# z of six head pairs of an attention layer as seven half-size products ahead of the attention loop

## The chip, the cores and the metric

The kernel runs on one core of one Trainium2 chip. The metric is device time in microseconds (us) of one execution. The engines are PE (TensorE, the matrix unit), DVE (VectorE), ACT (ScalarE), POOL (GpSimd) and SP (SyncE, which issues the DMA transfers). Each engine runs its own instructions in order and waits on semaphores for the others.

## What is computed

Two layers over 640 tokens: 512 of a prompt, and 8 samples of 16. Layer 0 is a gated MLP with a spatial mix (`gmlp_branch`); layer 1 is attention with a forget bias. The prompt attends to itself, the samples to 256 cached rows and to their own. z gates the attention's output by silu. Each layer ends with an output product, a residual with norms and a gated embedding. Cut to layer 1:

```python
proj = h @ w_in
q = proj[..., :E]; k = proj[..., E:2 * E]; v = proj[..., 2 * E:3 * E]
z = proj[..., 3 * E:4 * E]
logf = jax.nn.log_sigmoid(proj[..., 4 * E:] + b_f)
# prompt and samples, per head:
s = q @ k.T * scale + cT[q_pos] - cT[k_pos]      # cT: cumulative sum of logf
y = softmax(where(k_pos <= q_pos, s, -inf)) @ v
out = (y * jax.nn.silu(z)) @ w_out
```

D_MODEL is 1024, E 2048, and there are 16 heads of 128, worked on in eight pairs.

## The kernel before

**Products.** The precision is float32. Each operand is split into a high and a low fp32r part, and each product is three matmuls (`mm3`, L249 to L251: high by high, high by low, low by high). The activations of a layer, transposed and split, stand in A (`h_at`, `quarter`): 8 row tiles by 640 tokens. In the channel form (`channel_steps`) a 128x128 weight tile stands in PE and the 640 tokens pass in pieces of 384 and 256 columns.

**Seven products.** For a pair (256 output channels) the weights are cut into 2x2 blocks of four 128x128 tiles and the activations into 2x2 blocks of 320 tokens (`quarter`). `seven_products` (L523) forms the product of the two from seven products of blocks, or of sums of blocks, where the plain way takes eight: 7 x 4 tiles x 3 = 84 matmuls of 320 columns. The four sums of weights (left operands) are added by GpSimd in `left_operands` (L191 to L199); the sums of activations (right operands) are made once in `right_operands`, and the results are added on DVE (L531 to L546). Before, layer 0 alone does so, for its u and z.

**Weights.** `units` lists all weight pieces in the order of use. `fetch` loads them (512 KB each) into RAW, three slots. `split` makes the high part on ACT (L263) and the low part on DVE (L264) and puts them in W.

**Layer 1.** `project(p, parts)` makes v, k, q and z of head pair p. It is a generator, and `interleave` runs it and starts given pieces of attention at planned times. Pair 0 is projected first (with the forget logits, their logarithm and sums beside it). Then a loop over p = 0 to 6 projects pair p + 1 while pair p attends; the last pass has no z, since z of pair 7 is made behind the loop, with the last pair's attention and `tail(1)`, the output product. A pass of p = 0 to 5 has a planned length of 57 and steps of 5.6, the last one 43 and 4.2.

**Attention.** Per head, four row blocks of the prompt: scores on PE, softmax on DVE and ACT (its last step, the division by the row sum, is L955 before and L979 after), transposes on PE (L961 before, L985 after), values on PE (L968). For the samples, `load_k` brings cached K, 16 loads of 128 KB for a pair, and DVE transposes it (`turn_k`, L1000 before and L1024 after). K, V and the broadcast rows of c (the cumulative sums, through c_sc in DRAM) stand in one tile, r2b_t (`second`), 10240 columns wide. The results of a pair go to DRAM (y_sc) and come back for the tail.

**Queues.** Nearly all transfers are issued by SP (`dma`, L118 to L119), in order: a load that waits for its place holds up all that stand behind it. The scheduler that builds the program reorders instructions on each engine by its own estimate of time, so the order of rows decides what stands behind a wait.

Of the kernel before, what the change touches and what calls it, by code (L numbers as in the profile page):

```python
# [56 lines left out]
def hybrid_trunk(tc, x_prompt, x_sample, ck, cv, clf, p_prompt, p_sample, norm_pre, norm_post,  # L58
# [27 lines left out]
    c_sc = dram.tile([H, SEQ], F32, name="c_sc")  # L86
    cs_sc = dram.tile([P, 272], F32, name="cs_sc")
# [66 lines left out]
    for p in range(8):  # L154
        for part in (2, 1, 0, 3):
            for kk in range(2):
                u_rows(f_win[0], kk * 512, part * E + p * 256, 4, 256)
    u_tail(f_wout, 1)
# [15 lines left out]
    state = {"raw": 0, "used": 0}

    def raw_of(i):
        if S0 <= i < S1:
            z = (i - S0 + 1) % 4
            if z == NRAW:
                return r1(o_X, 1024)  # L180
        else:
            z = i % NRAW if i < S0 else (i + 1) % NRAW
        return RAW[:, z * 1024:z * 1024 + 1024]
# [7 lines left out]
    def left_operands(i, j):  # L191

        (a11, a21), (a12, a22) = ([raw_of(r).rearrange("p (k n) -> p k n", k=4)[:, :, z:z + P] for z in (0, P)] for r in (i, i + 1))
        s2, s3, s1, s4 = (SF[:, z * 512:z * 512 + 512].rearrange("p (k n) -> p k n", k=4) for z in range(4))
        if j == 0:
            for o, a, b, op in ((s1, a21, a22, ALU.add), (s2, s1, a11, ALU.subtract), (s3, a11, a21, ALU.subtract),
                                (s4, a12, s2, ALU.subtract)):
                nc.gpsimd.tensor_tensor(out=o, in0=a, in1=b, op=op)
# [186 lines left out]
    o_X, o_ln, o_sum, o_th = 14208, 15232, 16256, 17216  # L385
# [4 lines left out]
    SF = pool2.tile([P, 2560], F32, name="sf")  # L390

# [6 lines left out]
    b11, b12, b21, b22, t_a, t_b = (r1(10240 + z * 1280, 1280).rearrange("p (k n) -> p k n", k=4) for z in (0, 1, 2, 3, 4, 0))  # L398

    def right_operands():  # L400

        for q, (i, j) in zip((b11, b12, b21, b22), ((0, 0), (0, 1), (1, 0), (1, 1))):
            hi, lo = quarter(i, j)
            nc.vector.tensor_tensor(out=q, in0=f(hi), in1=f(lo), op=ALU.add)
        for o, a, b, dst in ((t_a, b12, b11, 0), (t_b, b22, t_a, 1), (b21, b21, t_b, 2), (b12, b22, b12, None)):
            nc.vector.tensor_tensor(out=o, in0=a, in1=b, op=ALU.subtract)
# [27 lines left out]
    for p in range(4):  # L434
# [4 lines left out]
        for kk in range(4):  # L439
# [20 lines left out]
    fetch(S0 + 4)  # L460
# [25 lines left out]
    assert o_A + 256 <= o_X  # L486
# [66 lines left out]

    def eight_products(done):
        wz = weights(2)
        for i in range(2):
            for j, o in enumerate(channel_unit(wz, i, UZ)):
                done(i, j, o[:, :HT])
# [32 lines left out]
    for g in range(0, 16, 2):  # L591
        for part, finish in ((0, finish_u), (1, finish_z)):
            if 2 * part in SEVEN:
                seven_products(lambda i, j: uv_of(g + i)[part][:, HALF[j]], lambda i, j, c: finish(g, i, j, c))
            else:
                eight_products(lambda i, j, c: finish(g, i, j, c))
# [174 lines left out]
    assert o <= 7168  # L771
# [112 lines left out]
    def project_q(p):  # L884
        ws = weights(2)
        for hh in range(2):
# [6 lines left out]
                                    scalar1=scale, scalar2=None, op0=ALU.mult)  # L893

# [258 lines left out]
```

## Time and profile before

| | |
|---|---|
| median of 3 runs (lowest to highest) | 1331.51 us (1331.37 to 1331.73) |
| the profiled execution: its own time | 1330.92 us |
| its span in the trace | 1329.1 us |
| busy: PE, DVE, ACT, POOL | 1319.5, 767.0, 542.6, 136.1 us |
| moved by DMA | 172.87 MB, 299913 packets, 188769 of them under 512 bytes |

The profile is one execution taken by the hardware profiler. PE is busy nearly all the time. Layer 0 reaches to about 540 us, pair 0 of layer 1 is projected up to about 600 us, the loop runs from there to about 1106 us, six passes of about 74 us and one of 60, and the rest is the last pair and the tail. PE's records of matmuls have modelled ends, so the time of one matmul is read from the distance of two starts. PEld is the loading of weights, which lies beside PE's work.

### The profile page before, as it was taken

How to read it: one execution, taken by the hardware profiler on the slowest of the kernel's cores; microseconds unless marked ns; L12 is line 12 of the kernel's file. 1: busy time of each engine (PE TensorE's matmuls, PEld its weight loads, DVE VectorE, ACT ScalarE, POOL GpSimd, SP SyncE). 2: the span in 40 equal slices, each digit the busy share in tenths (PEclk: the TensorE clock that was granted, in tenths of full speed). 3: DMA queues.
4: the chain of work that ended last, by engine and by line, in shares of the span. 5: the costliest groups of instructions: out<-in, count | busy, mean ns of one | idle time of the engine just before them, and what ended most of it. 6: DMA issues, size and time to landing. Idle time of an engine off the chain costs nothing.

```text
span 1329.1 us, 21541 instructions
## 1 busy us (share of the span) xinstructions
PE 1319.5 (99%) x8363; PEld 1191.4 (90%) x8363; DVE 767.0 (58%) x1581; ACT 542.6 (41%) x1025; POOL 136.1 (10%) x144
## 2 busy tenths in 40 slices
PE   9999999999999999999999999999999999999998
PEld 6888999999888788999999999999999998888786
DVE  7744999998844546545545454544545465544642
ACT  5434555444544334424333333433334344445341
POOL 1012454443000100000000000000000000000100
PEclk9999999999999999999999999999999999999999
DMA  6432343322424204689778675778778687243211
GB/s 224 137 101 69 119 129 102 106 85 73 139 86 151 79 26 120 184 141 170 124 163 165 153 165 140 157 153 163 122 148 173 149 211 244 92 149 112 64 64 48
DMA packets 299913, 172.87 MB, mean 130 GB/s; under 512 B 188769, under 2 KB 269201, under 8 KB 299810
## 3 DMA queue, kind: packets, MB, share of 16 engines
q1 hardware_dynamic: 299666, 171.23, 52.0%
q8 instruction: 65, 1.06, 0.3%
q14 instruction: 38, 0.31, 0.1%
q10 hardware_dynamic: 144, 0.26, 0.1%
HBM read 149.86 MB, written 21.59 MB: 129 GB/s over the span
## 4 chain that ended last, share of the span: by engine, by line
PE 97%; DVE 2%; DMA 0%; issue 0%; ACT 0%; SPq 0%; POOL 0%; DVEq 0%
PE pb L249 29%; PE pb L251 28%; PE pb L250 28%; PE pb L968 3%; PE pb L961 1%; PE pb L1022 1%; PE pb L1048 1%; PE pb L287 1%; PE pb L568 1%; DVE W L264 1%; PE pb L1045 1%; DMA RAW<-in_gmlp_w_in 0%; PE pb L1040 0%; DVE R L576 0%; PE pb L569 0%
## 5 line engine op out<-in xcount | busy, mean ns | idle before, releaser
L249 PE MATMUL pb<-A,W 128*128 128x384 f32 (+2 forms) x1024 | 330.4, 323 | 0.0
L251 PE MATMUL pb<-A,W 128*128 128x384 f32 (+2 forms) x1024 | 317.5, 310 | 0.0
L250 PE MATMUL pb<-A,W 128*128 128x384 f32 (+2 forms) x1024 | 316.8, 309 | 0.0
L249 PE MATMUL pb<-W,A 128*128 128x512 f32 (+1 forms) x840 | 298.2, 355 | 2.1 <-ACT R L694 1.4
L251 PE MATMUL pb<-W,A 128*128 128x512 f32 (+1 forms) x840 | 293.6, 351 | 0.6 <-DVE A L264 0.6
L250 PE MATMUL pb<-W,A 128*128 128x512 f32 (+1 forms) x840 | 294.1, 350 | 0.0
L264 DVE TENSOR_TENSOR W<-RAW,W 128x1024 fp32r<-128x1024 f32 (+1 forms) x156 | 193.2, 1239 | 151.2 <-ACT W L263 148.6
L263 ACT ACTIVATE W<-RAW 128x1024 fp32r<-128x1024 f32 (+1 forms) x156 | 161.2, 1033 | 155.4 <-PE pb L250 70.2
L249 PEld LDWEIGHTS pb<-A,W 128*128 128x128 f32 x1024 | 193.0, 188 | 7.5 <-issue 6.8
L250 PEld LDWEIGHTS pb<-A,W 128*128 128x128 f32 x1024 | 193.1, 189 | 0.7
L251 PEld LDWEIGHTS pb<-A,W 128*128 128x128 f32 x1024 | 192.6, 188 | 0.4 <-issue 0.4
L249 PEld LDWEIGHTS pb<-W,A 128*128 128x128 f32 x840 | 159.1, 189 | 26.5 <-issue 3.1
L251 PEld LDWEIGHTS pb<-W,A 128*128 128x128 f32 x840 | 158.9, 189 | 21.2 <-DVE A L264 0.9
L250 PEld LDWEIGHTS pb<-W,A 128*128 128x128 f32 x840 | 159.0, 189 | 20.1 <-issue 0.4
L264 DVE TENSOR_TENSOR A<-R,A 128x640 fp32r<-128x640 f32 (+1 forms) x51 | 41.0, 835 | 74.2 <-ACT A L263 71.9
L1000 DVE STREAM_TRANSPOSE r2b_t<-r2b_t 128x256 f32<-128x256 f32 x128 | 46.3, 412 | 34.4 <-PE pb L1022 26.1
L263 ACT ACTIVATE A<-R 128x640 fp32r<-128x640 f32 (+1 forms) x51 | 36.7, 747 | 67.6 <-PE pb L250 65.6
L249 PE MATMUL pb<-tb,W 128*128 128x320 f32 x192 | 59.7, 311 | 0.4
L251 PE MATMUL pb<-tb,W 128*128 128x320 f32 x192 | 59.3, 309 | 0.0
L250 PE MATMUL pb<-tb,W 128*128 128x320 f32 x192 | 59.3, 309 | 0.0
L273 POOL TENSOR_TENSOR SML<-SML 128x1 f32<-128x1 f32 x25 | 17.5, 701 | 385.4 <-DVE SML L271 380.7
L963 ACT ACTIVATE R<-pb 128x128 f32<-128x128 f32 (+1 forms) x64 | 27.9, 437 | 65.5 <-PE pb L961 65.3
(235 smaller groups left out, 1865.6 us busy)
## 6 DMA issues: line engine op xcount, KB each, us to landing
RAW<-in_fox_w_in SPq DMA_DIRECT2D x64, 512.0 KB
RAW<-in_gmlp_w_in SPq DMA_DIRECT2D x40, 512.0 KB
r2b_t<-in_cache_fox_v SPq DMA_DIRECT2D x32, 512.0 KB
r2b_t<-in_cache_fox_k SPq DMA_DIRECT2D x128, 128.0 KB
RAW<-in_gmlp_w_out SPq DMA_DIRECT2D x16, 512.0 KB
RAW<-in_ple_w_gate SPq DMA_DIRECT2D x16, 512.0 KB
RAW<-in_fox_w_out SPq DMA_DIRECT2D x16, 512.0 KB
out<-R SPq DMA_DIRECT2D x40, 128.0 KB
```

The lines of the kernel that those rows point to most:

```text
L249: nc.tensor.matmul(out, lh, rh, start=start, stop=False)
L250: nc.tensor.matmul(out, lh, rl, start=False, stop=False)
L251: nc.tensor.matmul(out, ll, rh, start=False, stop=stop)
L263: nc.scalar.activation(out=hi, in_=src, func=AF.Copy)
L264: nc.vector.tensor_tensor(out=lo, in0=src, in1=f(hi), op=ALU.subtract)
L273: nc.gpsimd.tensor_tensor(out=q, in0=t, in1=mhalf, op=ALU.pow)
L287: nc.tensor.transpose(out=b[:, j * P:(j + 1) * P], in_=src[:, (4 * c + j) * P:(4 * c + j + 1) * P], identity=ident)
L568: nc.tensor.matmul(b0[:, t * P:(t + 1) * P], v_at(pnl, t)[:, c0:c0 + P], wm, start=True, stop=True)
L961: nc.tensor.transpose(out=tb[:, j * P:(j + 1) * P], in_=pr[:, j * P:(j + 1) * P], identity=ident)
L963: nc.scalar.activation(out=pt[:, :n], in_=tb[:, :n], func=AF.Copy)
L968: nc.tensor.matmul(O[:, d], v[:, j, hh * P:(hh + 1) * P], pt[:, j * P:(j + 1) * P], start=(j == 0), stop=(j == i))
L1000: nc.vector.transpose(out=kt[:, hh, bl, :PAST], in_=kr[:, hh, bl])
```

## The change

z of pairs 1 to 6 is made by seven half-size products in `make_z`, pair after pair, ahead of the loop, and stored to DRAM (z_sc, 655 KB for a pair). `z_again` loads it in the pass that uses it, and the loop's projections have v, k and q alone; each pass has the length 43 and steps of 4.2. z of pair 0 is made by eight products as before, but right behind v and k, and q of pair 0 comes behind `make_z(6)`. z of pair 7 stays. In particular:

- `units` has the weights in the new order; `SEVEN` names two stretches of it where weights are split as sums and a fourth RAW slot is used.
- `right_operands` is called a second time, beside the projection of pair 0, with its four additions on GpSimd. It makes four sums (a fourth takes the place of a quarter that layer 0 replaces) in r2k_t, which stands where r2b_t stands later: r2b_t comes only when the last seven products have read it.
- The left sums go to R1, as do the forget gate's temporaries, which stood in r2b_t.
- The forget logits and their logarithm come at 24.0 and 30.0 of pair 0's projection and the sums behind z of pair 2. K of pair 0 is loaded in the first pass, not beside pair 0's projection.

```diff
-    for p in range(8):
-        for part in (2, 1, 0, 3):
+    def u_pair(p, parts):
+        for part in parts:
             for kk in range(2):
                 u_rows(f_win[0], kk * 512, part * E + p * 256, 4, 256)
+
+    u_pair(0, (2, 1, 3))
+    Z0 = len(units)
+    for p in range(1, 7):
+        u_pair(p, (3,))
+    Z1 = len(units)
+    u_pair(0, (0,))
+    for p in range(1, 8):
+        u_pair(p, (2, 1, 0) if p < 7 else (2, 1, 0, 3))
...
-    S0, S1 = 16, 48
-    SEVEN = (0, 2)
+    SEVEN = ((16, 48, 14208), (Z0, Z1, 13504))
...
-    def right_operands():
-
+    def right_operands(base, t3, eng):
+
+        b11, b12, b21, b22 = (r1(base + z * 1280, 1280).rearrange("p (k n) -> p k n", k=4) for z in range(4))
         for q, (i, j) in zip((b11, b12, b21, b22), ((0, 0), (0, 1), (1, 0), (1, 1))):
             hi, lo = quarter(i, j)
-            nc.vector.tensor_tensor(out=q, in0=f(hi), in1=f(lo), op=ALU.add)
-        for o, a, b, dst in ((t_a, b12, b11, 0), (t_b, b22, t_a, 1), (b21, b21, t_b, 2), (b12, b22, b12, None)):
+            eng.tensor_tensor(out=q, in0=f(hi), in1=f(lo), op=ALU.add)
+        for o, a, b, dst in ((b11, b12, b11, 0), (b12, b22, b12, t3), (b22, b22, b11, 1), (b21, b21, b22, 2)):
             nc.vector.tensor_tensor(out=o, in0=a, in1=b, op=ALU.subtract)
             if dst is not None:
                 split(*right_sum(dst), o)
+        return b12
...
-    pool2, R2 = second("r2b", F32)
+    pool2, TB = second("r2k", F32R)
+    state["sums"] = r1(10496, 2048)
...
+    def make_z(p):
+
+        zst = r1((7456, 15168)[p % 2], 2 * TOK)
+
+        def into(i, j):
+            return zst[:, i * TOK:(i + 1) * TOK][:, HALF[j]]
+
+        def done(i, j, c):
+            th = r1(14528 + j * HT, HT)
+            nc.scalar.activation(out=th, in_=c, func=AF.Tanh, scale=0.5)
+            nc.vector.scalar_tensor_tensor(out=into(i, j), in0=th, scalar=1.0, in1=c, op0=ALU.add, op1=ALU.mult)
+
+        seven_products(into, done, right_sum(3), 12544)
+        dma(z_sc[2 * p:2 * p + 2].rearrange("h p t -> p h t"), zst.rearrange("p (h t) -> p h t", h=2))
+
+    def z_again(p):
+        dma(r1(RA + (p % 2) * 4608 + 3328, 2 * TOK).rearrange("p (h t) -> p h t", h=2), z_sc[2 * p:2 * p + 2].rearrange("h p t -> p h t"))
...
-    PARTS = (project_v, project_k, project_q, project_z)
-    interleave(project(0, PARTS), [(0.0, forget_logits), (6.0, log_forget), (20.0, forget_sums), (30.0, lambda: load_k(0, 0))])
+    PARTS = (project_v, project_k, project_q)
+    interleave(project(0, (project_v, project_k, project_z)),
+               [(8.0, lambda: right_operands(12544, 3, nc.gpsimd)), (24.0, forget_logits), (30.0, log_forget)])
+    for p in range(1, 7):
+        make_z(p)
+        if p == 2:
+            forget_sums()
+    pool2.release()
+    pool2, R2 = second("r2b", F32)
+    run(project_q(0))
+    length, step = 43, 4.2
     for p in range(7):
-        length, step = (57, 5.6) if p < 6 else (43, 4.2)
-        pieces = kv_times(p, 0, 5) + kv_times(p, 1, length / 2) + sample_times(p, 0, 5) + sample_times(p, 1, length / 2)
-        pieces += [(2, lambda p=p: load_k(p, 1)), (length / 2 - 3, lambda p=p: load_k(p + 1, 0))]
+
+        t0, t1 = (12, 27) if p == 0 else (5, length / 2)
+        pieces = [(t0 - 14, lambda p=p: z_again(p))] if p else [(0, lambda: load_k(0, 0))]
+        pieces += kv_times(p, 0, t0) + kv_times(p, 1, t1) + sample_times(p, 0, t0) + sample_times(p, 1, t1)
+        pieces += [(t0 - 3, lambda p=p: load_k(p, 1)), (t1 - 3, lambda p=p: load_k(p + 1, 0))]
         for hh in range(2):
             pieces += prompt_times(2 * p + hh, 2 + 4 * step * hh, step)
-        interleave(project(p + 1, PARTS if p < 6 else PARTS[:3]), pieces)
+        interleave(project(p + 1, PARTS), pieces)
         store_y(p)
```

How the change moves rows is shown at two places (line, operation, tiles, shape; R_69 is the tile R1, pb is a PSUM bank, "waits" names the engine or DMA lane that a row waits for).

The first is SP's queue where the first cached K is loaded, before, beside pair 0's projection (c_sc and cs_sc hold the cumulative sums):

```order
L119 DMA r2b_t<-in_cache_fox_k 32x32x32 x4
L119 DMA RAW<-in_fox_w_in 128x4x256
L119 DMA r2b_t<-c_sc 128x512
L119 DMA R_69<-cs_sc 128x1x272
L119 DMA r2b_t<-in_cache_fox_k 32x32x32 x4
L119 DMA RAW<-in_fox_w_in 128x4x256
L119 DMA r2b_t<-c_sc 128x512
L119 DMA R_69<-cs_sc 128x1x272
```

and after, from the last weights of `make_z` to the first pass:

```order
L121 DMA RAW<-in_fox_w_in 128x4x256
L121 DMA r2b_t<-c_sc 128x512
L121 DMA r2b_t<-in_cache_fox_k 32x32x32 x5
L121 DMA z_sc<-R_69 128x2x640
L121 DMA r2b_t<-in_cache_fox_k 32x32x32 x3
L121 DMA r2b_t<-c_sc 128x512
L121 DMA r2b_t<-in_cache_fox_v 128x4x256 x2
L121 DMA RAW<-in_fox_w_in 128x4x256
L121 DMA r2b_t<-in_cache_fox_k 32x32x32 x4
L121 DMA r2b_t<-in_cache_fox_v 128x4x256
L121 DMA R_69<-z_sc 128x2x640
L121 DMA r2b_t<-in_cache_fox_k 32x32x32 x4
```

The sixteen K loads of pair 0, with c, V and the reload of z, now stand one behind the other behind the last product that reads r2k_t; before, they were spread over the projection of pair 0 and the first pass.

The second is DVE at the transposes of cached K. Before, the first ones stood beside splits of weights (L264) of pair 0:

```order
L264 TENSOR_TENSOR W<-R_69,W 128x512 [waits Activation_49]
L1000 STREAM_TRANSPOSE r2b_t<-r2b_t 128x256 [waits DMAHW2_49,DMAHW7_49,DMAHW1_49,DMAHW0_49]
L809 COPY r2b_t<-pb_74 16x512 [waits PE_49]
L819 COPY r2b_t<-pb_75 128x272 [waits PE_49]
L1000 STREAM_TRANSPOSE r2b_t<-r2b_t 128x256 [waits DMAHW2_49,DVE_49]
L1000 STREAM_TRANSPOSE r2b_t<-r2b_t 128x256
L264 TENSOR_TENSOR W<-RAW,W 128x1024 [waits DMAHW4_49,PE_49,Activation_49]
L1000 STREAM_TRANSPOSE r2b_t<-r2b_t 128x256 [waits DMAHW3_49,DVE_49]
L264 TENSOR_TENSOR W<-RAW,W 128x1024 [waits PE_49,Activation_49]
L1000 STREAM_TRANSPOSE r2b_t<-r2b_t 128x256 [waits DMAHW6_49,DMAHW7_49,DMAHW5_49,DMAHW0_49]
L1000 STREAM_TRANSPOSE r2b_t<-r2b_t 128x256
```

After, those for the second half of the samples stand between the parts of a softmax of the prompt (L975 to L979) and the samples' scores (L1049):

```order
L972 ISA SML 128x1
L975 TENSOR_SCALAR SML<-SML 128x1 [waits DVE_49]
L1024 STREAM_TRANSPOSE r2b_t<-r2b_t 128x256 [waits DMAHW4_49,DMAHW3_49,DMAHW5_49,DMAHW2_49,PE_49]
L978 RECIPROCAL SML<-SML 128x1 [waits Activation_49]
L1024 STREAM_TRANSPOSE r2b_t<-r2b_t 128x256 [waits PE_49] x3
L1024 STREAM_TRANSPOSE r2b_t<-r2b_t 128x256 [waits DMAHW2_49,DMAHW1_49,DMAHW3_49,DMAHW0_49,PE_49]
L979 TENSOR_SCALAR R_69<-R_69,SML 128x384 [waits DVE_49]
L1049 ISA R_69,SML<-pb_74,R_69 128x272 [waits PE_49,Pool_49]
L1049 ISA SML 128x1
L1024 STREAM_TRANSPOSE r2b_t<-r2b_t 128x256 x3
L279 TENSOR_TENSOR W<-RAW,W 128x1024 [waits Activation_49]
```

The division L979, which the transposes L985 on PE wait for, now has the last two groups of K transposes ahead of it, each with a wait for four DMA lanes; the next split of weights (L279, L264 before) stands behind them.

More of the change, by code (lines that the diff above doesn't have):

```diff
@@ L86, in hybrid_trunk @@
     c_sc = dram.tile([H, SEQ], F32, name="c_sc")
+    z_sc = dram.tile([H, P, TOK], F32, name="z_sc")
     cs_sc = dram.tile([P, 272], F32, name="cs_sc")
@@ L153, in hybrid_trunk @@
     u_tail(g_wout, 0)
-    for p in range(8):
-        for part in (2, 1, 0, 3):
+    def u_pair(p, parts):
+        for part in parts:
             for kk in range(2):
                 u_rows(f_win[0], kk * 512, part * E + p * 256, 4, 256)
+    u_pair(0, (2, 1, 3))
[6 more added lines that the diff above has]
+        u_pair(p, (2, 1, 0) if p < 7 else (2, 1, 0, 3))
+    n1 = len(units)
     u_tail(f_wout, 1)
-    S0, S1 = 16, 48
-    SEVEN = (0, 2)
+    SEVEN = ((16, 48, 14208), (Z0, Z1, 13504))
     items = []
+    raw_slot, raw_last = [], [-1] * (NRAW + 1)
+    part_of = {}
     for i in range(len(units)):
-        if not S0 <= i < S1 or i % 4 - i % 2 not in SEVEN:
+        part = next((x for x in SEVEN if x[0] <= i < x[1]), None)
+        if part is None:
             items.append((i, None))
-        elif i % 2 == 0:
+        elif i % 2 == part[0] % 2:
             items += [(i, j) for j in range(4)]
-    n0 = S1 + 16 + 2 + 8
-    few = range(n0, n0 + 64 + 12)
+            part_of[i] = part
+        if part and i == part[0]:
+            raw_last[NRAW] = i
+        z = min(range(NRAW + (part is not None)), key=lambda z: raw_last[z])
+        raw_last[z] = i
+        raw_slot.append(RAW[:, z * 1024:z * 1024 + 1024] if z < NRAW else r1(part[2], 1024))
+    few = range(Z1, n1 + 12)
     place, last_use = [], [-1] * (2 * NW)
-    state = {"raw": 0, "used": 0}
+    state = {"raw": 0, "used": 0, "sums": None}
     def raw_of(i):
[L177 to L183, printed above, removed]
+        return raw_slot[i]
     def fetch(upto):
@@ L193, in left_operands @@
         (a11, a21), (a12, a22) = ([raw_of(r).rearrange("p (k n) -> p k n", k=4)[:, :, z:z + P] for z in (0, P)] for r in (i, i + 1))
-        s2, s3, s1, s4 = (SF[:, z * 512:z * 512 + 512].rearrange("p (k n) -> p k n", k=4) for z in range(4))
+        sf = state["sums"]
+        s2, s3, s1, s4 = (sf[:, z * 512:z * 512 + 512].rearrange("p (k n) -> p k n", k=4) for z in range(4))
         if j == 0:
@@ L305, in hybrid_trunk, with channel_steps @@
     SPLITS = ((0, SA), (SA, TOK))
-    def channel_steps(ws, hh, banks, splits=SPLITS):
+    def channel_steps(ws, hh, banks):
         out = [bank(banks), bank(banks)]
@@ L311, in channel_steps @@
             w = [z[:, k % 4, hh * P:(hh + 1) * P] for z in ws[k // 4]]
-            for (a, b), o in zip(splits, out):
+            for (a, b), o in zip(SPLITS, out):
                 mm3(o[:, :b - a], w, h_at(k, a, b), k == 0, k == 7)
@@ L390, in hybrid_trunk @@
     SF = pool2.tile([P, 2560], F32, name="sf")
+    state["sums"] = SF[:, :2048]
     def quarter(i, j):
@@ L459, in hybrid_trunk @@
         load_ln(0)
-    fetch(S0 + 4)
+    fetch(20)
     mu, rs, shift = [], [], []
@@ L519, in y0_at, with seven_products @@
         return r1(g // 4 * 2560, 2560).rearrange("p (t n) -> p t n", t=NT)[:, :, (g % 4) * P:(g % 4 + 1) * P]
-    m1, u2, u3 = (r1(o_sum + z * HT, HT) for z in range(3))
     HALF = (slice(0, HT), slice(HT, TOK))
     UZ = (0, 1, 2, 3)
-    def seven_products(into, done):
-        rights = (quarter(0, 0), right_sum(1), quarter(0, 1), right_sum(0), quarter(1, 1), quarter(1, 0), right_sum(2))
+    def seven_products(into, done, t3, o_sum):
+        rights = (quarter(0, 0), right_sum(1), t3, right_sum(0), quarter(1, 1), quarter(1, 0), right_sum(2))
+        m1, u2, u3 = (r1(o_sum + z * HT, HT) for z in range(3))
         def total(i, j, a, b):
@@ L552, in seven_products @@
                 total(1, 0, u3, o)
[L554 to L558, printed above, removed]
     def gate_spatial(g):
@@ L592, in hybrid_trunk @@
         for part, finish in ((0, finish_u), (1, finish_z)):
[L593 to L596, printed above, removed]
+            seven_products(lambda i, j: uv_of(g + i)[part][:, HALF[j]], lambda i, j, c: finish(g, i, j, c), quarter(0, 1), o_sum)
             if part == 0:
```

19 lines of the change are left out of this document (8 added, 11 removed).

## The prediction, made before the run

> **What bounds the kernel now.** I read the page first: busy shares, slices, the chain that ended last.
>
> ```profile
> span 1329.1 us, 21541 instructions
> ...
> PE 1319.5 (99%) x8363; PEld 1191.4 (90%) x8363; DVE 767.0 (58%) x1581; ACT 542.6 (41%) x1025; POOL 136.1 (10%) x144
> ...
> PE   9999999999999999999999999999999999999998
> ...
> DMA  6432343322424204689778675778778687243211
> ...
> PE 97%; DVE 2%; DMA 0%; issue 0%; ACT 0%; SPq 0%; POOL 0%; DVEq 0%
> ```
>
> PE is busy for 1319.5 of 1329.1 us, no slice falls below nine tenths, and the chain lies on PE for 97%. So time goes only with PE work, and a gain survives only if DVE and the queue, which must do their share in less time, keep up. DMA is high (6 to 9 tenths) where the attention loop runs, so that loop comes next, in windows of one pass each (columns: length, PE, PEld, DVE, ACT, POOL with their instructions, clock, DMA share, GB/s):
>
> ```profile
> 1046.00:1106.00 60.00, 60.00 (x476) 56.32 (x475) 32.91 (x105) 25.37 (x58) 1.82 (x6) 1.00 0.83 196
> ...
> 972.00:1046.00 74.00, 74.00 (x572) 70.36 (x571) 36.01 (x110) 27.30 (x63) 1.53 (x6) 1.00 0.73 153
> 898.00:972.00 74.00, 74.00 (x572) 70.37 (x571) 36.02 (x110) 27.30 (x62) 2.32 (x6) 1.00 0.78 152
> 824.00:898.00 74.00, 74.00 (x572) 70.37 (x571) 36.01 (x110) 27.30 (x62) 2.15 (x6) 1.00 0.72 152
> 750.00:824.00 74.00, 74.00 (x571) 70.36 (x571) 36.03 (x110) 27.26 (x62) 2.35 (x6) 1.00 0.70 152
> 676.00:750.00 74.00, 74.00 (x571) 70.37 (x570) 36.02 (x110) 27.18 (x61) 1.39 (x6) 1.00 0.73 152
> 602.00:676.00 74.00, 74.00 (x571) 70.36 (x570) 36.04 (x110) 27.32 (x61) 1.63 (x6) 1.00 0.83 159
> ```
>
> PE is full in every pass, DVE half idle, the clock full. The top row is the last pass, which has no z and so the form that all passes get.
>
> **The products (the gain).** One product takes as long as the step to the next on PE's timeline (start, length, line, shape):
>
> ```profile
> 631.07 0.33 PE L249 MATMUL pb<-A,W 128*128 128x384 f32 x1
> ...
> 631.59 0.29 PE L249 MATMUL pb<-A,W 128*128 128x256 f32 x1
> ...
> 631.96 0.38 PE L1055 MATMUL pb<-CST,R 128*128 128x128 f32 x2
> 632.09 0.42 PE L249 MATMUL pb<-A,W 128*128 128x384 f32 x1
> 632.35 0.34 PE L250 MATMUL pb<-A,W 128*128 128x384 f32 x1
> ...
> 633.07 0.34 PE L249 MATMUL pb<-A,W 128*128 128x384 f32 x1
> ...
> 633.94 0.27 PE L939 MATMUL pb<-R 128*128 128x128 f32 x1
> ```
> ```profile
> 264.89 0.31 PE L249 MATMUL pb<-A,W 128*128 128x320 f32 x1
> ...
> 266.95 0.31 PE L251 MATMUL pb<-tb,W 128*128 128x320 f32 x1
> ```
>
> A weight tile of the channel form has three products of 384 columns and three of 256: 0.89 us from 631.07 to 631.96, 0.87 from 633.07 to 633.94, 0.88 in the mean. Fourteen steps of 320 columns take 2.06 us, 0.147 each. One pair's z is now 16 weight tiles, 14.1 us; as seven half-size products it is 84 products of 320, 12.35 us. Six pairs save 6 x 1.73 = **10.4 us** (9.4 to 11.3 by the rounding of the rows). Beside it, the first split product behind a plain one of attention takes 0.26 instead of 0.17 us (632.09 to 632.35), 0.09 a switch, and the order has 243 such switches where 248 were: **0.4 us**. All other matmuls stay the same in number and shape.
>
> **DVE beside the seven products.** One pair's z must fit 12.35 us on DVE, and GpSimd adds the left sums at the same time. The kernel has this already in layer 0:
>
> ```profile
> 218.00:246.00 28.00, 27.87 (x196) 27.59 (x195) 27.29 (x43) 12.81 (x24) 12.96 (x8) 1.00 0.37 109
> ```
> ```profile
> L264 DVE TENSOR_TENSOR W<-sf,W 128x1024 fp32r<-128x1024 f32 x21 | 25.6, 1217 | 1.9 <-ACT W L263 1.6
> L531 DVE TENSOR_TENSOR R<-R,pb 128x320 f32<-128x320 f32 x42 | 19.1, 477 | 0.7 <-PE pb L251 0.2
> L264 DVE TENSOR_TENSOR W<-RAW,W 128x1024 fp32r<-128x1024 f32 x11 | 17.4, 1577 | 3.3 <-ACT W L263 3.3
> L586 DVE SCALAR_TENSOR_TENSOR R<-sf,R 128x320 f32<-128x320 f32 x10 | 11.7, 1166 | 0.8 <-ACT sf L585 0.4
> ...
> L586 DVE SCALAR_TENSOR_TENSOR R<-R 128x320 f32<-128x320 f32 x10 | 4.9, 488 | 0.7
> ...
> L264 DVE TENSOR_TENSOR W<-RAW,W 128x512 fp32r<-128x512 f32 x5 | 3.4, 678 | 0.0
> ```
> ```profile
> L198 POOL TENSOR_TENSOR sf<-RAW,sf 128x512 f32<-128x512 f32 x10 | 20.0, 1998 | 0.8
> L198 POOL TENSOR_TENSOR sf<-RAW 128x512 f32<-128x512 f32 x9 | 12.4, 1379 | 45.6 <-DVE W L264 45.6
> ```
>
> (Groups of 190 to 330 us, about ten such products of eight weight tiles: busy sum and mean ns of one behind the bar.) DVE is 97% busy and PE loses 0.13 us in 28. Per z: two splits of sums 2.4, one of raw weights 1.6, a half one 0.7, seven additions 3.4, four gate operations of 0.49 to 1.17, half of each 3.3: 11.4 us, 92% of 12.35. I take a loss of nothing, since layer 0 hides the same load; bounds: 0.13 us per 28, 0.3 in all, and, if all four gate operations meet GpSimd (4.7, sum 12.8), 0.45 x 6 = 2.7 us. GpSimd's four additions per z take 1.4 to 2.0 each, at most 8 of 12.35.
>
> The Trainium skill (GPSIMD Engine Reference, 8. Key points) says that GpSimd shares its SBUF interfaces with VectorE and collides with VectorE instructions that have two SBUF inputs. The trace agrees: the split of raw weights, which stands beside the additions, takes 1577 ns where that of sums takes 1217; but it is a slowdown in part, with PE full, and not a turn for each.
>
> **The second right operands.** Their four additions of 1280 columns move to GpSimd: by 1379 to 1998 ns for 512, 3.4 to 5 us each, 14 to 20 together; four subtractions and four splits on DVE are
>
> ```profile
> L406 DVE TENSOR_TENSOR R<-R 128x1280 f32<-128x1280 f32 x4 | 5.8, 1480 | 0.0
> ...
> L264 DVE TENSOR_TENSOR tb<-R,tb 128x1280 fp32r<-128x1280 f32 x3 | 4.4, 1481 | 0.0
> ```
>
> 8 x 1.48 = 12 us. They are asked for at 8 and first needed behind v, k and z of pair 0, 3 x 14.0 = 42 us: 34 us for at most 32. Cost nothing; without that cover, what exceeds it, 0 to 2 us. ACT's shares and the forget sums, moved to pair 2's z, lie beside full PE as before: nothing, or 0.5 us.
>
> **The transition (the new wait).** The tile with the K and V caches and c takes the place of the one with the right sums, so none of its loads can start before the last seven-fold product. Before, the first ones came during project(0); on SP (issues) and DVE (in brackets: idle before, releaser):
>
> ```profile
> 563.81 3.45 SPq L119 DMA_DIRECT2D r2b_t<-in_cache_fox_k  x4
> ```
> ```profile
> 570.87 0.45 DVE L1000 STREAM_TRANSPOSE r2b_t<-r2b_t 128x256 f32<-128x256 f32 x1 [4.36 <-DMA r2b_t<-in_cache_fox_k]
> ...
> 579.48 0.77 DVE L1000 STREAM_TRANSPOSE r2b_t<-r2b_t 128x256 f32<-128x256 f32 x2 [2.56 <-DMA r2b_t<-in_cache_fox_k]
> ...
> 584.58 0.69 DVE L928 TENSOR_TENSOR r2b_t<-r2b_t,CST 128x512 f32<-128x512 f32 x1 [2.69 <-DMA r2b_t<-c_sc]
> ```
>
> DVE waited 9.6 us here with PE full. Now sixteen K loads, two of c, three of V, one of weights, a store and a reload of z come in one train. Prices: 10.4 us of queue (0.37 x 28) for 3.05 MB in the row 218:246, 3.4 us per MB; a pass has 0.748 x 74 = 55.4 us for 11.3 MB, of which 2.75 MB are in 128-byte packets (16 K loads of 131 KB and the k outputs), so (55.4 - 8.55 x 3.4) / 2.75 = 9.6 us per MB for these. The train is then 2.1 x 9.6 + (0.52 + 1.57 + 0.52 + 1.31) x 3.4 = 33.5 us; with a second or two of landing and gaps, 35 to 38 us after the last product. That price has a check: four K loads issued from 563.81 were there at 570.87, 7.1 us, against 5.0 plus the landing.
>
> DVE, in its order, has the last K transposes (L1024) ahead of a softmax division (L979) that PE's transposes (L985) wait for. Counted along PE's order by the prices above, these stand 34.9 us after the last 320-column product; between the landing and them lie five L1024 and L979, about 2 us. So PE waits 35 + 2 - 35 = 2 to 38 + 2 - 35 = 5 us: I take **3.5 us**, the middle. Bounds: nothing (loads in 31 us), and 8, where the split of weights that is queued behind on DVE comes late as well. The clock could add something after such a gap, but no row here shows a gap of this length in full work.
>
> The Trainium skill (DMA: Bandwidth & Descriptors, Why small descriptors are slow) gives a fixed overhead of about three cycles a packet beside one per 32 bytes: 7 cycles for 4 at 128 bytes, 1.75 times. By that (an estimate) K would cost 6 us per MB, the train 26 us, and the wait would be gone, the first rival's 1320.7 us. The rows bear out a factor near 2.8, so I stay with the wait.
>
> **The loops.** A pass loses 14.0 us of PE work and two weight units (1.05 MB, 3.6 us of queue) and gains a reload of z (0.66 MB, 2.2 us): 54.0 us of queue in 60.0 us, a share of 0.90; from the last pass before, 0.83 x 60 + 2.2 = 52.0, 0.87. Shares like these, with PE full:
>
> ```profile
> 610.00:620.00 10.00, 10.00 (x84) 10.00 (x83) 5.27 (x20) 4.16 (x11) 0.00 (x0) 1.00 0.99 180
> ...
> 1100.00:1110.00 10.00, 10.00 (x77) 9.43 (x76) 4.99 (x10) 2.88 (x5) 0.24 (x1) 1.00 0.97 331
> 560.00:630.00 70.00, 70.00 (x507) 66.30 (x507) 30.94 (x80) 23.79 (x47) 3.04 (x7) 1.00 0.88 156
> ```
>
> 0.88 held for 70 us, 0.99 for 10. I take no loss; each pass could lose 0 to 1 us where a load just misses its use.
>
> **Sum.** 1330.92 (the profiled execution's own time; 1329.1 span and 1.8 around it) - 10.4 - 0.4 + 3.5 = 1323.6. The median of the runs before is 0.6 higher, so I say **1324.2 us**.
>
> **Rivals.**
> - The wait is hidden: 1324.2 - 3.5 = 1320.7. For it: DVE's 9.6 us of waiting cost nothing before. Against it: the train's 33.5 us.
> - Smaller losses besides: z bound by DVE (2.7) or a late load in each pass (up to 6): 1326.5 to 1330.
> - Slower: SP's queue becomes the bound of the loops. It decides where a pass loses more than the 7.3 us of gain over six, 1.2 us, so where the share that the queue sustains is under 54.0 / 61.2 = 0.88. At 0.86 a pass takes 62.8 us, 2.8 x 6 = 17 more: 1341; at 0.83, the most of a whole pass so far, 65.1: 1355. For it: the queue is in order, and its loads wait for DVE to free tiles. Against it: the 0.88 above was no limit, since PE was full.
> - GpSimd and DVE take turns in z, 11.4 + 5.7 (12.96 of 28) = 17.1 us: 4.8 x 6 = 28 more, 1353. Layer 0's full PE with the same pairing leaves it 1 in 100.
> - That products stay as they are is excluded by the order: 504 more of 320 columns, 288 fewer each of 384 and 256.
>
> **How the numbers follow.** Forecast (wait of 2 to 5 us, 1322.5 to 1326) 0.46; hidden wait 0.24; smaller losses 0.20; slower loop or turns 0.10. The range takes in the first three: **1319.6 to 1331.5**. A measurement tells 0.2% (2.7 us) from no change. Faster, below 1328.8: the first two and two thirds of the third, 0.83; the same takes the rest of the third and a mild fourth, 0.10; slower 0.07.
>
> **What would show it.** In the profile after: 1848 products of 320 columns at 0.147; the six z near 74 us with PE full and DVE above 90%; behind them one PE gap of 2 to 5 us that L979 ends, with L1024 waiting for K; passes of 60 us with PE full and DMA near 0.9. A PE gap in each pass that a DMA ends would make me wrong upward, no gap behind the last z downward.

## The result: slower, by idle time at the start of layer 1

| | before | after |
|---|---|---|
| median of 4 runs (lowest to highest) | 1331.44 us (1331.05 to 1331.73) | 1337.74 us (1337.63 to 1338.21) |
| ratio after to before, 95% interval | | 1.0050 (1.0037 to 1.0062) |
| span of the profiled execution | 1329.1 us | 1335.9 us |
| PE busy; idle (span less busy) | 1319.5; 9.6 us | 1312.8; 23.1 us |

The forecast was 1324.2 us, between 1319.6 and 1331.5. The lines of the page of the changed kernel that answer to those of before:

```profile
span 1335.9 us, 21598 instructions
...
PE 1312.8 (98%) x8291; PEld 1182.5 (89%) x8291; DVE 831.3 (62%) x1643; ACT 561.2 (42%) x1047; POOL 183.1 (14%) x172
...
PE   9999999999999999889999999999999999999998
...
DMA  6432443322433214453598789998878889343211
...
PE 88%; DVE 4%; DMA 4%; issue 1%; SPq 1%; ACT 1%; POOL 0%; DVEq 0%; ACTq 0%; POOLq 0%
```

PE does 6.7 us less work, but is idle 13.5 us longer, which makes the 6.8 us of span. Two slices stand at 8, at about 530 to 600 us, and the chain now has 4% of DMA and 4% of DVE. The windows of the places where PE is idle, and two beside them for comparison (length, PE, PEld, DVE, ACT, POOL, clock, DMA share, GB/s):

```profile
540.00:600.00 60.00, 51.68 (x351) 48.10 (x349) 41.23 (x50) 23.72 (x38) 22.58 (x14) 0.97 0.49 94
...
602.00:676.00 74.00, 74.00 (x502) 72.83 (x501) 62.88 (x89) 32.64 (x51) 26.91 (x19) 1.00 0.52 130
...
700.00:720.00 20.00, 16.86 (x119) 15.69 (x119) 11.40 (x39) 7.96 (x19) 0.48 (x2) 0.91 1.02 199
760.00:800.00 40.00, 38.42 (x295) 36.03 (x294) 23.55 (x83) 16.26 (x40) 0.64 (x3) 1.00 0.82 203
...
860.00:920.00 60.00, 60.00 (x477) 56.32 (x476) 32.70 (x105) 24.52 (x57) 1.39 (x6) 1.00 0.96 189
```

Before, PE was full in all of these. Now 8.3 us are missing at 540 to 600, where layer 1 begins (pair 0's v, k and z), 3.1 at 700 to 720, the transition to the cache tile, and 1.6 at 760 to 800, in the first pass. The z products (602 to 676) and the later passes have no gap. The clock fell beside the first two: 3% of 60 us and 9% of 20 us are another 3.6 us.

**The largest loss.** Its parts are read on the queues, VectorE (DVE), GpSimd (POOL) and SP in turn; in brackets, the idle time before and what ended it:

```profile
554.53 0.44 DVE L279 TENSOR_TENSOR WF<-R,WF 128x128 fp32r<-128x128 f32 x1 [7.91 <-ACT WF L278]
...
556.12 0.68 DVE L279 TENSOR_TENSOR A<-pb,A 128x512 fp32r<-128x512 f32 x1
...
559.83 2.56 DVE L419 TENSOR_TENSOR R<-R 128x1280 f32<-128x1280 f32 x1 [2.30 <-POOL R L417]
562.31 4.59 DVE L279 TENSOR_TENSOR W<-RAW,W 128x1024 fp32r<-128x1024 f32 x2
```
```profile
550.69 2.91 POOL L417 TENSOR_TENSOR R<-A 128x1280 f32<-128x1280 f32 x1
553.56 1.26 POOL L213 TENSOR_TENSOR R<-R,RAW 128x512 f32<-128x512 f32 x1
...
556.87 2.92 POOL L417 TENSOR_TENSOR R<-A 128x1280 f32<-128x1280 f32 x1 [0.76 <-DVE A L279]
...
561.00 4.21 POOL L417 TENSOR_TENSOR R<-A 128x1280 f32<-128x1280 f32 x1
```
```profile
543.33 0.34 SPq L121 DMA_DIRECT2D x_sc<-R  x1
...
550.62 0.39 SPq L121 DMA_DIRECT2D R<-in_fox_w_in  x1
...
566.33 1.03 SPq L121 DMA_DIRECT2D RAW<-in_fox_w_in  x2
```

Two waits lie over each other. *First*, the forget gate's weights go to R1 at 4608, a place of layer 0's last token tile, so SP can load them only at 550.62, when that tile's store (543.33) has landed; ACT and DVE stand for 9.1 and 7.9 us at their two halves of that split (WF), and behind it on both stand the splits of the last token tile of h (A, on DVE at 556.12), which PE needs. *Second*, GpSimd's last three additions for the right operands (L417) start only at 550 to 561, with the first z's sums of weights (L213) between them. DVE's first subtraction (L419) waits for them until 559.83, and behind it stand two splits of weights (562.31). The first of the two, 128x1024, takes 3.99 us beside GpSimd's last addition, where such a split takes 1.22 otherwise. Only its end frees RAW, so that the next weights are issued at 566.33 instead of 557.49 as before.

### The profile page after: what moved, and what is told of

Same layout as the page of the kernel before. It is cut to its first block, busy times and chain, and to the rows that moved or that the text cites. A ratio compares the mean times of both kernels' runs of the same rounds, so it can differ in the third digit from the quotient of the medians.

```text
span 1335.9 us, 21598 instructions
## 1 busy us (share of the span) xinstructions
PE 1312.8 (98%) x8291; PEld 1182.5 (89%) x8291; DVE 831.3 (62%) x1643; ACT 561.2 (42%) x1047; POOL 183.1 (14%) x172
## 4 chain that ended last, share of the span: by engine, by line
PE 88%; DVE 4%; DMA 4%; issue 1%; SPq 1%; ACT 1%; POOL 0%; DVEq 0%; ACTq 0%; POOLq 0%
PE pb L264 26%; PE pb L266 26%; PE pb L265 26%; PE pb L992 3%; DMA RAW<-in_fox_w_in 2%; DVE W L279 2%; PE pb L985 1%; PE pb L1046 1%; SPq L121 1%; PE pb L1072 1%; PE pb L576 1%; PE pb L302 1%; DMA x_sc<-R 1%; PE pb L1069 0%; DMA RAW<-in_gmlp_w_in 0%
## 5 line engine op out<-in xcount | busy, mean ns | idle before, releaser
L264 PE MATMUL pb<-W,A 128*128 128x512 f32 (+1 forms) x840 | 299.2, 357 | 5.1 <-ACT A L278 3.8
L264 PE MATMUL pb<-A,W 128*128 128x320 f32 (+2 forms) x904 | 291.2, 322 | 3.2 <-DVE R L881 1.7
L266 PE MATMUL pb<-A,W 128*128 128x320 f32 (+2 forms) x904 | 280.9, 311 | 0.0
L265 PE MATMUL pb<-A,W 128*128 128x320 f32 (+2 forms) x904 | 280.4, 310 | 0.0
L279 DVE TENSOR_TENSOR W<-RAW,W 128x1024 fp32r<-128x1024 f32 x155 | 197.7, 1278 | 126.6 <-ACT W L278 123.1
L278 ACT ACTIVATE W<-RAW 128x1024 fp32r<-128x1024 f32 x155 | 157.8, 1019 | 148.6 <-PE pb L266 61.1
L264 PEld LDWEIGHTS pb<-W,A 128*128 128x128 f32 x840 | 159.8, 190 | 30.3 <-ACT A L278 4.5
L264 PEld LDWEIGHTS pb<-A,W 128*128 128x128 f32 x904 | 170.9, 189 | 11.2 <-issue 6.8
L265 PEld LDWEIGHTS pb<-A,W 128*128 128x128 f32 x904 | 171.0, 189 | 0.7
L266 PEld LDWEIGHTS pb<-A,W 128*128 128x128 f32 x904 | 170.6, 189 | 0.4 <-issue 0.4
L279 DVE TENSOR_TENSOR A<-R,A 128x640 fp32r<-128x640 f32 (+1 forms) x51 | 41.1, 835 | 72.0 <-ACT A L278 69.7
L264 PE MATMUL pb<-tb,W 128*128 128x320 f32 x192 | 59.7, 311 | 0.4 <-DVE R L557 0.3
L992 PE MATMUL pb<-R 128*128 128x128 f32 x320 | 46.5, 275 | 3.1 <-ACT R L987 3.1
```

Source lines behind the costliest of these rows:

```text
L264: nc.tensor.matmul(out, lh, rh, start=start, stop=False)
L265: nc.tensor.matmul(out, lh, rl, start=False, stop=False)
L266: nc.tensor.matmul(out, ll, rh, start=False, stop=stop)
L278: nc.scalar.activation(out=hi, in_=src, func=AF.Copy)
L279: nc.vector.tensor_tensor(out=lo, in0=src, in1=f(hi), op=ALU.subtract)
L992: nc.tensor.matmul(O[:, d], v[:, j, hh * P:(hh + 1) * P], pt[:, j * P:(j + 1) * P], start=(j == 0), stop=(j == i))
```

## Experiments

All are compared with the kernel before on the same chip (its medians there are 1331.2 to 1331.5 us); "both edits" means the first and the second one together.

**Constants elsewhere, additions on VectorE, both.** The edits:

```diff
-    o = 4608
+    o = 5120
...
-    cT, ex, cS = tmpa(SEQ, H), tmpa(P), tmpa(272)
+    cT, ex, cS = r1(4608, SEQ, H), tmpa(P), tmpa(272)
```
```diff
-               [(8.0, lambda: right_operands(12544, 3, nc.gpsimd)), (24.0, forget_logits), (30.0, log_forget)])
+               [(8.0, lambda: right_operands(12544, 3, nc.vector)), (24.0, forget_logits), (30.0, log_forget)])
```

> The forget gate's weights, bias and cached log values are loaded to columns 5120 to 5776 of R1 instead of 4608 to 5264, which the last token tile of layer 0 still occupies. Theory A (their loads wait for that tile's store, and VectorE stands with the last tile's splits behind): the PE gap of 3.6 us at 551 to 557 goes, and the lower clock behind it (1.7 us): 1331 to 1333 us against 1337.7 of the changed kernel. Theory B (the second right operands, with GpSimd's additions that VectorE waits for, cause the losses at the start of layer 1): no change, 1337 to 1338 us, gap still there or a few us later.

> The four additions of the second right operands run on VectorE instead of GpSimd, all else as in the changed kernel. Theory A: the gap at 551 to 557 stays (5.3 us with its clock); at most the smaller gaps at 575 to 600 (4.7 us of PE idle) go, so 1333 to 1337 us. Theory B: most of the 8 to 10 us at the start of layer 1 goes: 1328 to 1330 us.

> Both edits: constants at 5120 and additions on VectorE. If each causes its own gaps (A for 551 to 557, B for 575 to 600), the whole loss at the start of layer 1 goes, about 10 us: 1327 to 1329 us, and the losses left are the one at 708 to 716 and the one at 776 to 792. If the gaps at 575 to 600 only follow from the late weights of the first one, the result is that of the first edit alone.

| kernel | median (lowest to highest) | ratio to before, 95% interval |
|---|---|---|
| constants elsewhere | 1337.16 us (1336.04 to 1338.09) | 1.0046 (1.0029 to 1.0063) |
| additions on VectorE | 1329.13 us (1326.01 to 1329.82) | 0.9980 (0.9970 to 0.9991) |
| both | 1326.02 us (1325.97 to 1326.46) | 0.9960 (0.9946 to 0.9975) |

Theory A alone fails, and theory B's times hold: moving the additions back brings 8.6 us. The first kernel's trace shows why the constants alone bring nothing. DVE and windows of it:

```profile
558.95 2.57 DVE L419 TENSOR_TENSOR R<-R 128x1280 f32<-128x1280 f32 x1 [9.02 <-POOL R L417]
561.44 4.58 DVE L279 TENSOR_TENSOR W<-RAW,W 128x1024 fp32r<-128x1024 f32 x2
```
```profile
570.00:580.00 10.00, 3.55 (x21) 3.27 (x20) 5.75 (x5) 4.51 (x6) 0.00 (x0) 0.69 0.67 91
580.00:590.00 10.00, 10.00 (x58) 10.00 (x57) 9.93 (x13) 4.17 (x6) 4.93 (x4) 0.79 0.47 86
```

The 7.9 us of waiting at WF are gone, and DVE waits 9.0 us at L419 instead; PE's idle moves from 551 to 570 and beyond. The second wait lay hidden under the first.

What of this delays the weights shows beside the kernel with both edits, whose text differs from this one's by the additions' engine alone. The split by its shape and GpSimd's last addition here, then the split with both edits:

```profile
L279 DVE TENSOR_TENSOR W<-RAW,W 128x1024 fp32r<-128x1024 f32 x1 | 4.0, 3983 | 0.0
```
```profile
560.13 4.21 POOL L417 TENSOR_TENSOR R<-A 128x1280 f32<-128x1280 f32 x1
```
```profile
559.94 1.22 DVE L279 TENSOR_TENSOR W<-RAW,W 128x1024 fp32r<-128x1024 f32 x1
```

The next weights are issued at 565.45 here and at 561.18 with both edits, 4.3 us apart. Only 1.5 of these come from the later start of the split (561.44 against 559.94), since with both edits DVE spends much of that time on the additions itself; 2.8 come from the split itself, 3.98 us against 1.22. It ends at 565.4, 1.1 us after GpSimd's addition (564.3), as if it had stood until that was done. So the two engines' hold on each other costs the weights more than the wait in DVE's order does.

The edit of the additions also changes the scheduler's order on PE: ahead of the last token tile's transposes PE gets twelve more products of 384 columns (2.1 us). With the additions on VectorE DVE still waits 5.5 us at WF, but PE idles only 0.3 us near 555 instead of 3.6 at 551 to 557, against theory A's expectation; at 575 to 600 it idles 1.3 us instead of 4.7.

With the additions on DVE the constants' edit brings 1329.1 to 1326.0, 3.1 us, a microsecond more than its expectation allowed. The profiled executions show 1.5 us of idle less at 540 to 600; another 2.0 lie at 700 to 720, where the constants take no part, and the eight runs without them spread from 1326.0 to 1329.8, so that only the 1.5 can be put down to their wait. In the kernel with both edits the stretch is full:

```profile
540.00:600.00 60.00, 60.00 (x422) 57.30 (x422) 49.59 (x59) 26.21 (x41) 19.81 (x13) 1.00 0.46 99
700.00:720.00 20.00, 18.46 (x145) 16.47 (x146) 13.56 (x45) 10.04 (x24) 0.00 (x0) 1.00 0.78 131
760.00:780.00 20.00, 16.02 (x127) 13.86 (x127) 10.12 (x34) 6.43 (x16) 0.40 (x2) 1.00 0.98 238
```

What is left is at the transition (1.5 us here) and in the first pass (4.0).

**Subtractions later.** Could GpSimd keep the additions if DVE's subtractions stood behind its splits?

```diff
-               [(8.0, lambda: right_operands(12544, 3, nc.gpsimd)), (24.0, forget_logits), (30.0, log_forget)])
+               [(28.0, lambda: right_operands(12544, 3, nc.gpsimd)), (24.0, forget_logits), (30.0, log_forget)])
```

> Constants at 5120 as in the first experiment; the additions stay on GpSimd, but the second right operands are asked for at 28 of pair 0's projection instead of 8, so that on VectorE their subtractions stand behind the splits of weights and not ahead of them. Theory B1 (what costs is VectorE's queue: its first subtraction waits for GpSimd with splits of weights behind it): the loss at the start of layer 1 goes almost as with the additions on VectorE, 1326 to 1329 us. Theory B2 (what costs is that both engines slow each other down: additions of 2.9 to 4.2 us, splits of 2.3): most of the loss stays, 1332 to 1337 us.

1340.62 us (1338.62 to 1342.45), ratio 1.0070 (1.0055 to 1.0085): a miss of both. GpSimd's additions now stand behind a new wait, on the stores of k, whose buffer they overwrite, and DVE stands behind GpSimd:

```profile
576.02 5.77 POOL L417 TENSOR_TENSOR R<-A 128x1280 f32<-128x1280 f32 x2 [17.85 <-DMA out<-R]
```
```profile
578.99 6.62 DVE L419 TENSOR_TENSOR R<-R 128x1280 f32<-128x1280 f32 x2 [7.82 <-POOL R L417]
```

So the run does not tell the wait in DVE's queue from the mutual slowing of the two engines, though it shows the slowing again (two subtractions, 1.48 us each where GpSimd is idle, take 6.62 here; the expectation's splits of 2.3 are the mean of the 3.98 above and of a half-wide one of 0.6). It shows once more that whatever holds GpSimd holds DVE, and with it the weights.

**Weights further ahead (the transition).**

```diff
-            fetch(u + 1 if j is None else u + 2)
+            fetch(u + 1 if j is None and u < Z1 else u + 2)
```

> Weights from q of pair 0 on are fetched one unit further ahead, so that one weight load stands ahead of the last four K loads in SP's queue; all else as in the changed kernel. Theory C (PE's gap at 708 to 716, 3.1 us and 1.7 us of clock, comes from a weight load that is queued behind the K train, ScalarE standing at its split): that gap goes or halves, 1332.5 to 1335.5 us. Theory D (the prediction's: VectorE's K transposes hold the softmax division): the K loads land no earlier, the gap stays, 1337 to 1339 us.

1341.29 us (1339.58 to 1342.31), ratio 1.0073 (1.0058 to 1.0088). In the changed kernel the gap at 708 to 715 ended with ScalarE's split of weights, which were issued at 703.97, behind the last K loads; the transpose's copy L987, which PE waits for, stood behind it:

```profile
712.23 1.06 ACT L278 ACTIVATE W<-RAW 128x1024 fp32r<-128x1024 f32 x1 [7.22 <-DMA RAW<-in_fox_w_in]
713.19 0.36 ACT L987 ACTIVATE R<-pb 128x256 f32<-128x256 f32 x1
```

With one weight load ahead of them, ScalarE is in time, but DVE waits for the last K loads:

```profile
711.92 0.45 DVE L1024 STREAM_TRANSPOSE r2b_t<-r2b_t 128x256 f32<-128x256 f32 x1 [7.01 <-DMA r2b_t<-in_cache_fox_k]
```

PE is idle 3.6 us between 700 and 720, no less than 3.1. Both theories fall short: theory C names the wait of the changed kernel, but the order in the train only chooses who waits; that its amount sets the gap is what the next runs test. (Its other loss against the changed kernel lies elsewhere: 2.7 us of idle at 760 to 800 instead of 1.6, and a clock of 0.91 there and at 540 to 600, a stretch ahead of the edit.)

**K ahead, no detour of z, z ahead without the seven products.** The amount was tried from two sides, on the kernel with both edits. The first eight K loads of pair 0 are issued behind the forget sums, into R1:

```diff
-        kr = r2(o_K, 2048).rearrange("p (h b n) -> p h b n", h=2, b=4)
+        kr = (r1(4608, 2048) if i == 0 else r2(o_K, 2048)).rearrange("p (h b n) -> p h b n", h=2, b=4)
...
             forget_sums()
+            load_k(0, 0)
...
-        pieces = [(t0 - 14, lambda p=p: z_again(p))] if p else [(0, lambda: load_k(0, 0))]
+        pieces = [(t0 - 14, lambda p=p: z_again(p))] if p else []
```

> The kernel with both edits (constants at 5120, additions on VectorE: 1326.0 us), and the first eight K loads of pair 0 go to columns 4608 to 6656 of R1, free behind the forget sums, so that they come beside the z products and not behind them: the train is eight loads (10 us of queue) shorter. Theory C' (the train's length sets the 1.8 us of PE idle near 700 and, by what it leaves behind, the 4.0 us near 760 to 780): both go, 1320 to 1322 us. Rival: the pass itself has too much for the queue, and the losses come back in later passes: 1324 to 1326 us.

Here pair 1's v is written to K's place before K is read, so that four samples of pair 0 are computed from other data. 1322.35 us (1320.27 to 1323.91), ratio 0.9932 (0.9917 to 0.9947). The time lies between the two expectations: no idle is left at 700 to 720, but 1.6 of the 4.0 us at 760 to 780 stay. The other side leaves out the two transfers of z:

```diff
-        dma(z_sc[2 * p:2 * p + 2].rearrange("h p t -> p h t"), zst.rearrange("p (h t) -> p h t", h=2))
...
-        pieces = [(t0 - 14, lambda p=p: z_again(p))] if p else [(0, lambda: load_k(0, 0))]
+        pieces = [] if p else [(0, lambda: load_k(0, 0))]
```

> The kernel with both edits, without the stores of z to DRAM and without the reloads, so that pairs 1 to 6 are gated by what stands in the place of z: 7.9 MB less for the queue. If the detour through DRAM is what the first passes lack, the 5.8 us near 700 and 760 to 780 go for the most part: 1320 to 1323 us; if the K loads alone make the train, 1 to 2 us at most go: 1324 to 1326 us.

1321.38 us (1320.50 to 1321.89), ratio 0.9927 (0.9910 to 0.9944): as its first expectation has it. The detour costs about 4.6 us here, and no idle is left in these two places. The third kernel takes the right sums away and makes z of pairs 1 to 6 in the channel form:

```diff
-    SEVEN = ((16, 48, 14208), (Z0, Z1, 13504))
+    SEVEN = ((16, 48, 14208),)
...
-        seven_products(into, done, right_sum(3), 12544)
+        ws = weights(2)
+        for i in range(2):
+            for (a, b), ps in zip(SPLITS, run(channel_steps(ws, i, UZ))):
...
-               [(8.0, lambda: right_operands(12544, 3, nc.vector)), (24.0, forget_logits), (30.0, log_forget)])
+               [(24.0, forget_logits), (30.0, log_forget)])
```

> The kernel with both edits, but z of pairs 1 to 6 ahead of the loop by eight products in the channel form, without right operands and sums of weights; nothing reads the tile of the right sums, so the tile of the caches is free from the start and there is no train. By the prediction's terms PE's work is that of before less the switches, and no transition: 1330.9 - 0.4, 1330 to 1331 us. If the passes without z and with z's reload are bound by SP's queue even without a train, they are longer than 60 us: 1333 us or more.

1342.77 us (1341.52 to 1343.57), ratio 1.0085 (1.0070 to 1.0100). The time lies in the second expectation's range, but not for its reason: at 800 to 1100 the passes without z are full (0.4 us of idle in all). Both expectations are wrong on the cause. There is a train after all, only earlier: with the tile free from the start, the K loads go among the first weights of layer 1. SP and ScalarE:

```profile
566.99 2.59 SPq L121 DMA_DIRECT2D r2b_t<-in_cache_fox_k  x3
...
570.32 1.01 SPq L121 DMA_DIRECT2D RAW<-in_fox_w_in  x2
```
```profile
580.57 1.06 ACT L278 ACTIVATE W<-RAW 128x1024 fp32r<-128x1024 f32 x1 [9.33 <-DMA RAW<-in_fox_w_in]
```

Weights that take 10 us to land hold ScalarE's split for 9.3 us, and PE idles 7.0 us from 540 to 700.

**K ahead in a free place; z of pair 1 kept.** The eight loads go to 5888 and 16448 of R1; then, besides, z of pair 1 is written where its pass reads it:

```diff
-        kr = r2(o_K, 2048).rearrange("p (h b n) -> p h b n", h=2, b=4)
+        kr = [(r1((5888, 16448)[h], 1024) if i == 0 else r2(o_K + h * 1024, 1024)).rearrange("p (b n) -> p b n", b=4) for h in range(2)]
```
```diff
-        zst = r1((7456, 15168)[p % 2], 2 * TOK)
+        zst = r1(7936 if p == 1 else (15168, 4608)[p % 2], 2 * TOK)
...
+        if p > 1:
+            dma(z_sc[2 * p:2 * p + 2].rearrange("h p t -> p h t"), zst.rearrange("p (h t) -> p h t", h=2))
```

> As the experiment with K ahead, but the eight loads go to columns 5888 to 6912 and 16448 to 17472 of R1, which pair 1's v, written before the transposes, does not take. Theory C' as before: the PE idle near 700 (1.8 us with both edits) is gone, that near 760 to 780 is 1 to 2 us instead of 4.0: 1321 to 1323 us. If the first placing was fast only because v took the place of K, the time is that with both edits, 1326 us.

> As the run before, and z of pair 1 is written to its final place and neither stored nor loaded again: 1.3 MB or 4.4 us of queue less, most of it in the first pass. If the queue's work in the first pass makes the idle near 760 to 780, that goes too: 1319.5 to 1321.5 us. If it is the order of the transfers and not their amount, no change against the run before.

1321.17 us (1320.98 to 1321.85), ratio 0.9925 (0.9911 to 0.9940), and 1320.96 us (1319.87 to 1321.78), ratio 0.9925 (0.9908 to 0.9941). The first computes all that the kernel before does and is faster than it by 10.0 us, near the 10.8 that the forecast had for the products and switches. Its page and windows:

```profile
PE 1308.8 (99%) x8291; PEld 1180.1 (89%) x8291; DVE 829.1 (63%) x1647; ACT 561.4 (43%) x1047; POOL 171.5 (13%) x168
```
```profile
700.00:720.00 20.00, 20.00 (x160) 18.26 (x159) 11.45 (x42) 7.84 (x19) 0.40 (x2) 1.00 0.72 118
760.00:800.00 40.00, 40.00 (x313) 37.23 (x312) 20.89 (x65) 15.91 (x35) 0.86 (x4) 1.00 0.96 176
860.00:920.00 60.00, 60.00 (x478) 56.32 (x477) 32.79 (x106) 24.06 (x55) 1.39 (x6) 1.00 0.96 201
```

The first lies in its expected range, so the earlier placing was not fast only because v took K's place. Nothing was left for the second to save at 760 to 800, so its expectation could not be tested; the two times do not differ.

## Why the prediction was wrong

- **The products: right.** PE's busy time with the eight K loads in a free place is 1308.8 us, 10.7 less than before, against 10.8 forecast; in the other kernels with the additions on VectorE it is 1306.6 to 1309.4. In the changed kernel only 6.7 of it show, since 4.0 us (0.3% of the span, by the mean clock of 0.997) went to the lower clock.
- **DVE beside the seven products: right.** DVE is busy for 62.88 of 74 us there, 85%, and PE for all of them; the forecast had 92% and no loss.
- **The second right operands: the step that failed.** "Cost nothing; without that cover ... 0 to 2 us" compared 32 us of work with 34 us of time up to the first use. It counted durations, not what stands beside and behind them. GpSimd's additions of 2.9 to 4.2 us each end only at 564 to 565, as two of them need the last token tile, which DVE splits at 549 to 557 us, and the first z's sums of weights stand between them. DVE waits for them with weights' splits behind it, and a split beside them takes 4.0 us instead of 1.2; it frees RAW late, and the next weights come late. Measured: 8.6 us for the edit that moves the additions back. The prediction had DVE's 1.48 us from rows in which GpSimd is idle, and left out here the collision of the two engines that it had named for z; there it had called it a slowdown in part, "not a turn for each", while the split here ends as if it had waited for its turn. Of the rivals, that of smaller losses named other places, and none had this one.
- **The moved temporaries: not priced.** The sum had "nothing, or 0.5 us" for the forget gate's part and looked at its instructions alone. The tile that its loads go to changed, and with it what they wait for: 3.1 us by the medians once the other wait is gone, of which 1.5 show as idle time in its stretch. Without the other edit it brings only 0.6 us. The two edits together took 11.7 us, from 1337.7 to 1326.0.
- **The transition: the train right, the wait wrong, its size luck.** The last K was at DVE 34.3 us after the last 320-column product (started at 673.16), against 35 to 38 forecast:

```profile
707.48 0.45 DVE L1024 STREAM_TRANSPOSE r2b_t<-r2b_t 128x256 f32<-128x256 f32 x1 [4.20 <-DMA r2b_t<-in_cache_fox_k]
707.85 0.38 DVE L979 TENSOR_SCALAR R<-R,SML 128x384 f32<-128x384 f32 x1
```
```profile
709.10 0.49 PE L985 MATMUL pb<-CST,R 128*128 128x128 f32 x3
...
713.61 0.71 PE L992 MATMUL pb<-R 128*128 128x128 f32 x4 [3.14 <-ACT R L987]
```

PE reaches the transposes L985 after L979 is done and does not wait: the forecast wait is nothing. The 3.1 us come at L992, from the weights behind the train and ScalarE's split; the forecast had a late split only on DVE, and only in its bound of 8. So 3.1 us against 3.5 is luck, and 1.8 us of clock, named in the forecast without a price, come on top. The price of 9.6 us per MB for K gave a train of 33.5 us, close to the 34.3; the estimate by the Trainium skill (DMA: Bandwidth & Descriptors, Why small descriptors are slow) gave 26 us and no gap. The measurement is nearer to the first, though the queue was not full all the time (a share of 0.80 from 673 to 690, 1.08 from 690 to 707).
- **The loops: right but for the first pass.** Passes at shares of 0.84 to 0.96 are full, so the rival of a queue as the bound of the loops is false. The first pass has the rest of the train on top and loses 1.6 us here, 4.0 with both edits; the forecast's "0 to 1 us where a load just misses its use" was too small for this pass and too large for the others.

Not settled: how the 8.6 us divide between the wait in DVE's order, the slow split and the other order on PE. The traces give the first two their shares of the weights' delay (1.5 and 2.8 us), but no run has one without the others, and the run that was to part them brought a wait of its own. Why the gap at the transition differs between kernels with the same train (3.2 us with the additions on VectorE, 1.5 with both edits) is open too.

## What to carry to other kernels

Where work is moved to an idle engine, it is not enough to set its duration against the time to its first use. Ask when its last operand comes, what stands behind the instruction that waits for its result, and what it does to the engine that works beside it; then follow that engine's queue to the weights and to PE. A temporary that moves to another tile brings that tile's last reader as a new wait. Behind one late wait a second may lie hidden, so an edit that brings nothing alone is to be tried again together with the next.

## What the runs showed of the hardware

PE's granted clock fell to half after some gaps. Windows of the changed kernel, and of the one with the constants elsewhere:

```profile
550.00:554.00 4.00, 2.27 (x14) 1.95 (x12) 0.00 (x0) 0.00 (x0) 4.00 (x3) 1.00 0.36 42
554.00:558.00 4.00, 2.13 (x11) 1.81 (x12) 2.99 (x5) 2.04 (x5) 3.24 (x3) 0.90 0.31 55
558.00:562.00 4.00, 4.00 (x26) 4.00 (x25) 2.17 (x1) 2.07 (x3) 4.00 (x3) 0.67 0.00 0
```
```profile
574.00:578.00 4.00, 0.00 (x0) 0.00 (x0) 3.75 (x4) 3.00 (x5) 0.00 (x0) 0.50 0.71 85
```

A gap of 3.0 us is followed by 4 us at 0.67 in the mean; the one of 6.5 us brought 0.50 while PE was idle. The length of a gap alone does not decide it. The clock also fell after gaps of 3.1 us (at the transition of the changed kernel, 0.80 over 716 to 720), 3.8 us (without the seven products, 0.50 over 582 to 586) and once after one of 2.0 us (weights further ahead, 0.50 over 780 to 786). It did not fall after one of 3.2 us (at the transition with the additions on VectorE), nor after one of 2.0 with both edits. The Trainium skill (TensorE: Matmul & The Clock Gate, HAM oscillation — how this bites in real kernels) warns of gaps above about 3.4 us, at which the clock goes to half; the runs agree in the 0.50, but here it fell after shorter gaps too. Where it fell, 3.6 us of idle at 551 to 557 were worth 5.3: 4 us at 0.90 and 4 us at 0.67 are another 1.7.

A DVE instruction with both inputs in SBUF and a GpSimd addition held each other up. Alone, a split of 128x1024 takes 1.22 us, a subtraction of 128x1280 1.48 and GpSimd's addition of 128x1280 2.9; side by side at 559 to 566 they took 3.98, 2.57 and 4.21.
